# Two encoder layers on one core: the latent heads' first score products are kept in PSUM, their maxima are taken from them by DVE, and the list of the stage is made by readiness

## The chip, the core and the metric

The program runs on one core of a Trainium2 chip. A core has five engines that run their own lists in order and wait for each other by semaphores: TensorE (PE; its weight loads are shown as PEld), VectorE (DVE), ScalarE (ACT), GpSimd (POOL) and SyncE (SP, which here only issues transfers). PE writes to PSUM, which this kernel uses as eight banks of 128 x 512 float32. The metric is the device time of one execution in microseconds (us), as a median over runs.

## The reference

Two layers over 512 tokens of width 1024, batch 1, float32. Each layer normalises its input, projects it, and runs three branches that are merged by gates; then a gated MLP follows. What bears on the change is the first branch, attention from latents with 8 heads of width 96 (64 plain and 32 rotary), cut to its core:

```python
q = (rms_norm(c_q, q_norm_g) @ w_uq).reshape(b, s, MLA_HEADS, MLA_QK)
kv = (rms_norm(c_kv, kv_norm_g) @ w_ukv).reshape(b, s, MLA_HEADS, MLA_NOPE + MLA_V)
k_nope, v = kv[..., :MLA_NOPE], kv[..., MLA_NOPE:]
k = jnp.concatenate([k_nope, k_rope], axis=-1)      # k_rope: one for all heads
q, k = rms_norm(q, qh_g), rms_norm(k, kh_g)         # then axial rotary on the last 32
sc = jnp.einsum('bqgrd,bkgd->bgrqk', q, k) * 96 ** -0.5
p = jax.nn.softmax(sc, axis=-1)
o = jnp.einsum('bgrqk,bkgv->bqgrv', p, v)
# merged = sum over branches of sigmoid(gate) * (o @ w_branch);  x = x + merged @ w_out
# x = x + (silu(conv(hf @ w_up)_gate) * conv(hf @ w_up)_val) @ w_down
```

The second branch is grouped-query attention with 8 heads of width 64 ("gqa" in the code), the third a pooling branch.

## The kernel before

All activations lie with features on partitions and the 512 tokens along the free axis. Every float32 operand is split into a high part that PE takes exactly and a low remainder (ACT copies the high part, DVE or POOL subtracts), and a product is three PE products: high by high, high by low, low by high (`mm3`). Weights stream from HBM through three raw tiles, are split on the core (ACT `wh`, POOL or DVE `wl`), and are used once.

The list of every engine is fixed when the program is built. A small planner, `Clock` (line 133), keeps a model of the time at which each engine is free and each value ready. `chain` (line 184) puts a series of steps on the engines one after another; `Engine` prices each step (0.07 us plus 0.00105 us per element for a DVE step with two inputs, a reduction or a turn; 0.00053 per element for a DVE copy in SBUF), and `mm` prices a product at columns/2370 us, which is 0.216 us for 512. `copy` (line 507) takes ACT or DVE, whichever the model has free sooner, and `pick` does so for DVE and POOL.

The attention of a layer is made by `attention(kind, fill, ...)` (line 1150), first for "gqa", then for "mla", the latent heads. Between its products PE takes units of `fill`: products of the gates and of the branch projections, three 512-wide products a unit, in the two banks called acc. For the latent heads the filler is `fb` (line 1460): the rest of the second branch and the first 48 units of the first branch's gates. What is left of the first branch follows the attention (`rest[0].finish()`, line 1465).

A latent head h goes through these steps:

- `go_turn`: DVE turns 32x32 blocks of the head's q and k (`block_turn`, line 1117; source tiles MQ and MK), SP writes them out and reads them back with features on partitions (`tf`), and a constant `pad` fills partitions 96 to 127: zeros for q, and for k a row of ones at 96 and zeros below it.
- `t_q`, `t_k`: ACT and POOL split them: `qa`, `qb` (high and low of q), `kh`, `kl` (high and low of k; `ka`, `kb` inside the head's record).
- `s_max(h, b)` (line 1232), four times: one product with queries on partitions, `qa` block by `kh`, into the one bank S; DVE reduces it to the negated maximum over keys (`nm`). After the fourth, DVE turns the four columns into `nmt`, and ACT copies them in four steps into partitions 96 to 127 of `qa`.
- `probs(h, k)` (line 1264), four times: three products with keys on partitions, into a bank ST or mi. The ones of the k pad times the maxima in `qa` subtract the maximum inside the product. Then ACT takes the exponential in place (`ex`), ACT or DVE makes the high part `ph`, DVE the low part `pl`, and one value step (`rest`, into `vt`) adds what the 128-column value product leaves out; then the bank is free.
- `av_hi`, `av_lo`, `av_rest`: products with the values into a bank AV; then `o_out` (line 1335) evacuates (ACT), and for each pair of heads the sums are turned, inverted and multiplied (`osum`, `oinv`, `oraw`), and split into `oh`, `ol`.

The order of these steps on PE comes from `PLAN` (line 47): for each kind of head, fixed positions of each step relative to the head's place, in quarters of a head; filler is spread over the positions, and where a step would wait by the model, up to `SLACK` units of filler are taken early. `nbank` (line 297) gives the banks: acc 2, S 1, ST 2, AV 2, mi 1.

The norm of a layer's input (`norm_begin`, line 474) has DVE turn the summed squares into `sqT` and reduce them to `prt`.

Of the kernel before, what the change touches and what calls it, by code (L numbers as in the profile page):

```python
# [13 lines left out]
AF = mybir.ActivationFunctionType  # L14
# [32 lines left out]
PLAN = {"gqa": (-4.2, -1.0, -0.2, 0.0, 0.65, 2.411, 4.57, 32.003),  # L47
        "mla": (-6.2, -2.9, -1.0, 0.1, 0.64, 1.678, 1.82, 35.5)}
# [85 lines left out]
class Clock:  # L134
# [5 lines left out]
    def __init__(self):  # L140
        self.now, self.n, self.heap, self.busy = 0.0, 0, [], False
        self.fin, self.free, self.ready = 0.0, {}, {}
        self.source = self.last = None

# [39 lines left out]
    def chain(self, *steps, after=0.2):  # L184

        def go(n, source=None):
# [77 lines left out]
def trunk(ctx: ExitStack, tc: tile.TileContext, x, w, prm, gb, cst, pad, out):  # L264
# [3 lines left out]
    at, need, done, chain = ck.at, ck.need, ck.done, ck.chain  # L268
# [49 lines left out]
    def f(ap):  # L318
        return ap.bitcast(F32)
# [154 lines left out]
    def norm_begin(gen, sq):  # L474

        t, part = slot("sqT"), small("prt", [P, 16])
# [72 lines left out]
    def layer(l, sq, xsrc):  # L549
# [204 lines left out]
        def set_keys():  # L754
            for _, kb in KAB:
                G.memset(f(kb[64:P, :T]), 0.0)
                G.memset(f(kb[64:65, :T]), 1.0)
# [128 lines left out]

        def gates(br, okey, odst, mode):
            hold = {}

            def gate(m):  # L890
                tag = "AV" if br == 2 and m < 2 else "acc"
                acc = ps(tag)
                yield from feat_major(acc, G1)
                t = hold[m] = slot("gt")

                def logits():
                    V.tensor_tensor(t[:, :T], acc, nrm["rbc"][:, :T], ALU.mult)
                    free(tag)

                chain(([("rbc", G1)], logits), lambda: A.activation(t[:, :T], t[:, :T], AF.Tanh, scale=0.5))  # L900

            def branch(m):
# [22 lines left out]

                if mode == "first":
                    chain(product)
                elif mode == "add":
                    chain(product, add)
                else:  # L930
                    mh, ml = slot("mgh", F32R), slot("mgl", F32R)
                    merged[m] = (mh, ml)
                    chain(product, add, *split(mh[:, :T], ml[:, :T], XM[:, m, :]), fin)
# [47 lines left out]
        def q_out(g, b, acc):  # L981
# [10 lines left out]
            chain(copies, lambda: A.activation(j[:, :384], MQ[g][:, b].rearrange("p h f -> p (h f)"), AF.Square), sums)  # L992
# [55 lines left out]
        def n_out(g, p, acc):  # L1048
# [7 lines left out]
            def sums():  # L1056
# [4 lines left out]
                                               MK[g][:, bs, :, 0:64], AF.Square), sums)  # L1061
# [55 lines left out]
        def block_turn(what, h, srcs, n, rest=None):  # L1117
# [24 lines left out]
            return turn_blocks, put, get  # L1142
# [7 lines left out]
        def attention(kind, fill, okey, odst):  # L1150
# [5 lines left out]

            def t_q(h):
# [7 lines left out]
                def lo():  # L1165
# [3 lines left out]
                chain(lambda: A.activation(qf[:, :T], qf[:, :T], AF.Copy, scale=gcol),  # L1169
                      lambda: A.activation(qa[:, :T], qf[:, :T], AF.Copy), lo, after=0.0)  # L1170
# [92 lines left out]

            def probs(h, k):
# [10 lines left out]
                else:  # L1275
                    mm(sc, s["kb"][:, kb_], s["qa"][:, :T], True, False)
                    mm(sc, s["ka"][:, kb_], s["qb"][:, :T], False, False)
                    mm(sc, s["ka"][:, kb_], s["qa"][:, :T], False, True)
                ph, pl = slot("ph", F32R), slot("pl", F32R)
# [13 lines left out]
                def rest():  # L1293
# [8 lines left out]
                    free(tag)  # L1302
                    if k == 3:
                        done(*key("t", h))

                chain(ex, hi, lo, ([("vg", l, k) if gqa else ("vm", l, k, h // 4)], rest))
# [22 lines left out]
            def av_rest(h):  # L1329
                s = hs[h]  # L1330
                need(key("t", h))
                mm(s["av"], unit, s["t"][:, :T], False, True)
                o_out(h)

            def o_out(h):
# [26 lines left out]
                steps = [copies]  # L1362
                if h % 2 == 1:
# [4 lines left out]
                    steps += [lambda: V.transpose(turned[:, :T], sums[:, :T]),  # L1368
# [3 lines left out]
                    steps += [lambda: V.transpose(sums[:, :T].rearrange("p (b f) -> p b f", f=32),  # L1372
                                                  bc(inv.unsqueeze(2), [P, 16, 32]))]
# [4 lines left out]

            plan = []
# [15 lines left out]
            def waits(fn, h, k=None):  # L1395
# [15 lines left out]
                return [key("t", h)] if fn is av_rest else [key("pl", h, k)], None  # L1411
# [50 lines left out]
        while not ck.has(("tq", l, 0)) and fb.step():  # L1462
            pass
        attention("mla", fb, "om", omla)
# [311 lines left out]
```

## Time and profile before

| | |
|---|---|
| median of three runs | 1565.33 us (1565.16 to 1565.37) |
| span of the profiled execution | 1562.8 us (the page gives its time as this span) |
| instructions | 20576, of them 7098 PE products |
| PE busy | 1556.6 us |
| POOL, DVE, ACT busy | 1035.8, 946.2, 821.5 us |
| granted TensorE clock | 1.000 |
| latent heads, layer 0 | 230.4 to 342.8 us |
| latent heads, layer 1 | 1005.6 to 1118.0 us |

The page names an instruction by line, engine, operation and tiles, output first. Nearly every step here is recorded by a helper (line 379 is every product, 225 every ACT step, 232, 236, 240, 244, 248 and 256 the kinds of DVE and POOL steps), so one goes by the tiles: `nm`, `qb`, `ph`. PE products are pipelined: the length shown of one, 390 ns, is more than the distance from one to the next.

### The profile page before, as it was taken

The page shows a single profiled execution, that of the slowest core. Times are in us where ns is not written, and L with a number is a line of the kernel's source. Part 1 is how long each engine was busy: PE and PEld are TensorE (multiplying, and loading weights), DVE is VectorE, ACT ScalarE, POOL GpSimd, SP SyncE. Part 2 cuts the span into 40 slices and gives each one's busy share as a digit, 9 for nine tenths or more (in the row PEclk, how much of TensorE's full clock was granted, in tenths as well). Part 3 has the DMA queues.
Part 4 walks back from the last instruction along what each step waited for, and adds up shares of the span by engine and source line. Part 5 has one row for each costly group of instructions (what it writes and reads, how often), then busy time and mean ns, then how long its engine had stood idle before and what let it go on. Part 6 is the DMA issues. An engine that isn't in the chain of part 4 may idle for free.

```text
span 1562.8 us, 20576 instructions
## 1 busy us (share of the span) xinstructions
PE 1556.6 (100%) x7098; PEld 1301.2 (83%) x7098; DVE 946.2 (61%) x1377; ACT 821.5 (53%) x1538; POOL 1035.8 (66%) x922
## 2 busy tenths in 40 slices
PE   9999999999999999999999999999999999999999
PEld 8888788888888888888898888888888888888888
DVE  6778877865266777711046788788562767776000
ACT  6558777863444444432244687788533444444221
POOL 4975985854667666664578669867546676666542
PEclk9999999999999999999999999999999999999999
DMA  6432234325323323333335322443242222322331
GB/s 208 125 109 75 75 117 151 111 68 149 96 93 108 95 94 95 95 120 111 112 105 135 95 77 73 141 137 101 82 149 94 94 95 95 107 95 95 108 130 46
DMA packets 82856, 166.48 MB, mean 107 GB/s; under 512 B 20928, under 2 KB 42944, under 8 KB 82752
## 3 DMA queue, kind: packets, MB, share of 16 engines
q1 hardware_dynamic: 82464, 165.03, 33.8%
q8 instruction: 56, 0.92, 0.2%
q14 instruction: 48, 0.39, 0.1%
q10 hardware_dynamic: 288, 0.14, 0.0%
HBM read 151.50 MB, written 13.63 MB: 106 GB/s over the span
## 4 chain that ended last, share of the span: by engine, by line
PE 97%; POOL 2%; issue 0%; DMA 0%; ACT 0%; SPq 0%; DVE 0%; POOLq 0%
PE ps_acc L379 44%; PE ps_AV L379 23%; PE ps_ST L379 22%; PE ps_mi L379 3%; PE ps_S L379 3%; POOL MQ L232 0%; DMA XM<-x 0%; POOL wl L232 0%; POOL oraw L232 0%; POOL qb L232 0%; POOL qa L232 0%; SPq L330 0%; SPq L1606 0%; POOL rp L232 0%; ACT HH L225 0%
## 5 line engine op out<-in xcount | busy, mean ns | idle before, releaser
L232 POOL TENSOR_TENSOR wl<-raw,wh 128x512 fp32r<-128x512 f32 (+3 forms) x503 | 675.4, 1355 | 369.5 <-ACT wh L225 336.4
L225 ACT ACTIVATE wh<-raw 128x512 fp32r<-128x512 f32 (+2 forms) x521 | 308.2, 607 | 124.8 <-PE ps_ST L379 42.7
L236 DVE SCALAR_TENSOR_TENSOR a<-u,prm,a 128x511 f32<-128x511 f32 x176 | 243.1, 1384 | 91.8 <-ACT a L225 87.8
L379 PE MATMUL ps_acc<-HH,wh 128*128 128x512 f32 x592 | 231.1, 390 | 0.1
L379 PE MATMUL ps_acc<-HL,wh 128*128 128x512 f32 x592 | 230.9, 390 | 0.0
L379 PE MATMUL ps_acc<-HH,wl 128*128 128x512 f32 x592 | 230.8, 390 | 0.0
L379 PEld LDWEIGHTS ps_acc<-HH,wl 128*128 128x128 f32 x592 | 111.2, 188 | 23.3
L379 PEld LDWEIGHTS ps_acc<-HH,wh 128*128 128x128 f32 x592 | 111.3, 188 | 22.8 <-issue 0.4
L379 PEld LDWEIGHTS ps_acc<-HL,wh 128*128 128x128 f32 x592 | 111.2, 188 | 22.6
L232 POOL TENSOR_TENSOR al<-a,ah 128x512 fp32r<-128x512 f32 x44 | 58.1, 1320 | 83.5 <-ACT ah L225 81.4
L379 PE MATMUL ps_AV<-HH,wh 128*128 128x512 f32 x288 | 112.4, 390 | 0.0
L379 PE MATMUL ps_AV<-HH,wl 128*128 128x512 f32 x288 | 112.2, 390 | 0.0
L379 PE MATMUL ps_AV<-HL,wh 128*128 128x512 f32 x288 | 112.2, 390 | 0.0
L240 DVE TENSOR_REDUCE nm<-ps_S 128x1 f32<-128x512 f32 x128 | 87.6, 684 | 37.0 <-PE ps_S L379 36.5
L225 ACT ACTIVATE ah<-a 128x512 fp32r<-128x512 f32 x44 | 27.8, 632 | 128.1 <-DVE a L232 128.1
L379 PE MATMUL ps_ST<-HH,wh 128*128 128x512 f32 x240 | 93.6, 390 | 0.0
L379 PE MATMUL ps_ST<-HL,wh 128*128 128x512 f32 x240 | 93.5, 390 | 0.0
L379 PE MATMUL ps_ST<-HH,wl 128*128 128x512 f32 x240 | 93.5, 389 | 0.0
L225 ACT ACTIVATE a<-u,prm 128x512 f32<-128x512 f32 x88 | 71.0, 809 | 23.8 <-DVE u L232 23.5
L225 ACT ACTIVATE a<-a 128x512 f32<-128x512 f32 x44 | 27.6, 632 | 104.4 <-DVE a L236 104.3
L225 ACT ACTIVATE HH<-XM,prm 128x512 fp32r<-128x512 f32 x32 | 23.1, 722 | 102.9 <-DVE XM L232 53.9
L225 ACT ACTIVATE ps_ST<-ps_ST 128x512 f32<-128x512 f32 x86 | 50.1, 583 | 28.5 <-PE ps_ST L379 28.4
(387 smaller groups left out, 3752.3 us busy)
## 6 DMA issues: line engine op xcount, KB each, us to landing
raw<-w SPq DMA_DIRECT2D x228, 512.0 KB, 3.5
raw<-w SPq DMA_DIRECT2D x13, 384.0 KB, 3.1
XM<-x SPq DMA_DIRECT2D x16, 256.0 KB, 3.8
dtq<-tr SPq DMA_DIRECT2D x16, 192.0 KB, 1.9
dtk<-tr SPq DMA_DIRECT2D x16, 192.0 KB, 2.2
tf<-dtq SPq DMA_DIRECT2D x48, 64.0 KB, 2.2
tf<-dtk SPq DMA_DIRECT2D x48, 64.0 KB, 2.1
raw<-w SPq DMA_DIRECT2D x6, 448.0 KB, 3.4
```

The lines of the kernel that those rows point to most:

```text
L225: return self.eng.activation(out, in_, func, **k)
L232: return self.eng.tensor_tensor(out, *a)
L236: return self.eng.scalar_tensor_tensor(out, *a)
L240: return self.eng.tensor_reduce(out, in_, *a, **k)
L379: PE.matmul(o, lhsT=lhsT, rhs=rhs, start=start, stop=stop)
```

## The change

Only the latent heads and the norm's reduction are rewritten; grouped-query heads keep `PLAN` and `s_max`.

- `a_part(h, k)` takes the place of `s_max` and of one of the three products of `probs`: high by high, keys on partitions, into one of the banks ST, ST, mi, S, or one of the two AV banks if no other score holds one. The bank is kept. DVE reduces each bank with a reduction that turns 32x32 blocks (`largest`), so that the maximum over 32 keys of a query lands on a partition; after the fourth, `over_keys` (a small reduction over the four banks), `gather` (three DVE copies of 16 elements, from the other groups of 32 partitions to partitions 96 to 127), `over_groups` (a small reduction, negated) and `row` (a DVE product of that with a 32x32 identity, 32 x 512, into partitions 96 to 127 of `qb`).
- `pad` for k is ones in all 32 rows, so that the product of k with the diagonal blocks in `qb` subtracts each query's maximum.
- `b_part(h, k)` adds the other two products to the bank (high k by `qb`, low k by `qa`), then the same steps as before (`weights`). The value steps of one head now wait for each other in the planner's order.
- `held_banks` takes the place of the fixed positions: it goes over a list of tasks, in order of heads, and issues the first that the model has ready, with a margin (0.1 us for `a_part`, 0.4 for `b_part`, 1.2 for the value products); if none is, a unit of filler. A head's first `a_part` waits until a share of the filler is done, with 22 units left for after the last head's start.
- `low` and `way` mark steps that give way in the planner: if their engine is busy by the model, they are put off, up to 4 us (1 us for the filler's bank steps, 1.5 for the evacuation of values).
- `norm_begin` uses one reduction that turns, in place of turn and reduction.

```diff
-PLAN = {"gqa": (-4.2, -1.0, -0.2, 0.0, 0.65, 2.411, 4.57, 32.003),
-        "mla": (-6.2, -2.9, -1.0, 0.1, 0.64, 1.678, 1.82, 35.5)}
+PLAN = {"gqa": (-4.2, -1.0, -0.2, 0.0, 0.65, 2.411, 4.57, 32.003)}
+LEAD = {"mla": (1.2, 22)}
...
+    def low(self, fn, most=4.0, engine="DVE"):
+        self.gives_way[fn] = (engine, most)
+        return fn
...
+            eng, most = self.gives_way.get(fn, (None, 0.0))
+            since = self.now if since is None else since
+            if self.free.get(eng, 0.0) > self.now + 0.02 and self.now < since + most:
+                self.at(self.free[eng] - self.now, lambda: go(n, source, since))
+                return
...
-        chain(([("sq", gen, kc) for kc in range(KC)], lambda: V.transpose(t[:, :T], sq[:, :T])),
-              lambda: V.tensor_reduce(part, t[:, :T].rearrange("p (j r) -> p j r", r=32), AX.X, ALU.add),
+        chain(([("sq", gen, kc) for kc in range(KC)], lambda: V.tensor_reduce(
+            part, sq[:, :T].rearrange("p (j r) -> p j r", r=32), AX.X, ALU.add, apply_transpose=True)),
...
+        def way(br, fn, most=4.0):
+            return low(fn, most) if now_mla[0] else fn
...
+            def a_part(h, k):
+                s = hs[h]
+                tag, sc = sc_bank()
+                s["sc", k] = (tag, sc)
+                PE.matmul(sc, lhsT=s["ka"][:, k * P:k * P + P], rhs=s["qa"][:, :T], start=True, stop=True)
...
+                def largest():
+                    V.tensor_reduce(s["pm"][:, k], sc.rearrange("p (j r) -> p j r", r=32), AX.X, ALU.max,
+                                    apply_transpose=True)
+
+                def over_keys():
+                    s["row"] = small("mrow", [P, 16], bufs=1)
+                    V.tensor_reduce(s["pk"][:, 3], s["pm"].rearrange("p k j -> p j k"), AX.X, ALU.max)
+
+                def gather():
+                    for g in range(4):
+                        if 32 * g != base:
+                            V.tensor_copy(s["pk"][base:base + 32, g if g < 3 else base // 32], s["pk"][32 * g:32 * g + 32, 3])
+
+                def over_groups():
+                    V.tensor_reduce(s["row"][base:base + 32], s["pk"][base:base + 32].rearrange("p g j -> p j g"), AX.X, ALU.max,
+                                    negate=True)
+
+                def row():
+                    V.tensor_tensor(s["qb"][base:base + 32, :T].rearrange("p (j r) -> p j r", r=32),
+                                    bc(s["row"][base:base + 32].unsqueeze(2), [32, 16, 32]),
+                                    bc(ident[base:base + 32, None, base:base + 32], [32, 16, 32]), ALU.mult)
+                    done(*key("m", h))
+
+                chain(largest, *[over_keys, gather, over_groups, ([key("q", h)], row)] * (k == 3), after=0.3)
+
+            def b_part(h, k):
+                s = hs[h]
+                need(key("m", h), key("q", h))
...
+                pairs = [("kb", "qb")] if gqa else [("kb", "qa"), ("ka", "qb")]
+                for n, (a_, b_) in enumerate(pairs):
+                    PE.matmul(sc, lhsT=s[a_][:, kb_], rhs=s[b_][:, :T], start=False, stop=n == len(pairs) - 1,
+                              skip_group_check=True)
+                    ck.to(ck.now + T / 2370.0)
+                weights(h, k, sc, lambda: sc_free(tag))
...
-                chain(ex, hi, lo, ([("vg", l, k) if gqa else ("vm", l, k, h // 4)], rest))
+                chain(ex, hi, lo, ([("vg", l, k) if gqa else ("vm", l, k, h // 4)] + [key("t", h, k - 1)] * (k > 0), rest))
...
+            def held_banks():
...
+                lead, late = LEAD[kind]
+                step = (fill.total - fill.done - late) / 7.0
...
+                    for k in range(4):
+                        task(a_part, h, k, keys=[key("q" if gqa else "qh", h)] + [key("kh", h)] * (not gqa), margin=0.1, bank="sc",
+                             after=[(t_q, h - h % 2 if gqa else h)] + [(b_part, h - 1, 3)] * (h > 0) + [(t_k, h)] * (not gqa)
+                             + [(a_part, h, k - 1)] * (k > 0), fills=f0 + step * h if k == 0 else 0)
+                    for k in range(4):
+                        task(b_part, h, k, keys=[key("m", h), key("q", h)] + [key("kl", h)] * (not gqa), margin=0.4,
+                             after=[(b_part, h, k - 1) if k else (a_part, h, 3)])
...
+                while todo:
+                    for n, z in enumerate(todo):
+                        if can(*z):
+                            todo.pop(n)
+                            z[0](*z[1])
+                            issued.add((z[0],) + z[1])
+                            break
+                    else:
+                        if not fill.step():
+                            ck.to(ck.now + 0.05)
+                fill.finish()
...
-        "pad": np.stack([np.zeros((32, T), np.float32), np.eye(32, 1, dtype=np.float32) * np.ones(T, np.float32)]),
+        "pad": np.stack([np.zeros((32, T), np.float32), np.ones((32, T), np.float32)]),
```

More of the change, by code (lines that the diff above doesn't have):

```diff
@@ L267, in trunk @@
     ck = Clock()
-    at, need, done, chain = ck.at, ck.need, ck.done, ck.chain
+    at, need, done, chain, low = ck.at, ck.need, ck.done, ck.chain, ck.low
     V, A, G = Engine(ck, nc.vector, "DVE"), Engine(ck, nc.scalar, "ACT"), Engine(ck, nc.gpsimd, "Pool")
@@ L924, in fin @@
                     done("mrg", l, m)
+                way(br, product, 1.0)
                 if mode == "first":
@@ L990, in sums @@
                 done("ssq", l, g, b)
-            chain(copies, lambda: A.activation(j[:, :384], MQ[g][:, b].rearrange("p h f -> p (h f)"), AF.Square), sums)
+            chain(copies, lambda: A.activation(j[:, :384], MQ[g][:, b].rearrange("p h f -> p (h f)"), AF.Square), way(0, sums))
         def q_norm(g):
@@ L1140, in get @@
                 done(what, l, h)
-            return turn_blocks, put, get
+            return way(0, turn_blocks), put, get
         def mla_turn(what, h):
@@ L1155, in key, with sc_tags, sc_ready, sc_bank @@
                 return (kind, l) + k
+            held = [0]
+            def sc_tags():
+                return ("ST", "mi", "S") + ("AV",) * (held[0] == 0)
+            def sc_ready():
+                return any(banks[t] and banks[t][0] <= ck.now for t in sc_tags())
+            def sc_bank():
+                while not any(banks[t] for t in sc_tags()):
+                    ck.pop()
+                tag = min((t for t in sc_tags() if banks[t]), key=lambda t: max(banks[t][0], ck.now) + 0.01 * (t == "AV"))
+                held[0] += tag == "AV"
+                return tag, ps(tag)
+            def sc_free(tag):
+                held[0] -= tag == "AV"
+                free(tag)
             def t_q(h):
@@ L1278, in probs, with weights @@
                     mm(sc, s["ka"][:, kb_], s["qa"][:, :T], False, True)
+                weights(h, k, sc, lambda: free(tag))
+            def weights(h, k, sc, release):
+                s = hs[h]
                 ph, pl = slot("ph", F32R), slot("pl", F32R)
@@ L1360, in add @@
                     G.tensor_tensor(raw[:, :T], raw[:, :T], sums[:, :T], ALU.add)
-                steps = [copies]
+                steps = [low(copies, 1.5, "ACT") if kind in LEAD else copies]
                 if h % 2 == 1:
@@ L1379, in attention @@
+            if kind not in PLAN:
+                held_banks()
+                return
             plan = []
```

74 lines of the change are left out of this document (59 added, 15 removed).

## Prediction

> **What bounds the kernel now.** I read the page's busy times and its chain first, then the chain in order of time, then windows over the two latent-attention stages, and there what TensorE's weight loads wait for. First the busy times and the chain's shares by engine, from the page.
>
> ```profile
> PE 1556.6 (100%) x7098; PEld 1301.2 (83%) x7098; DVE 946.2 (61%) x1377; ACT 821.5 (53%) x1538; POOL 1035.8 (66%) x922
> PE 97%; POOL 2%; issue 0%; DMA 0%; ACT 0%; SPq 0%; DVE 0%; POOLq 0%
> ```
>
> PE is never free and 97% of the chain is PE: time is the number of products times their rate. The chain in order of time (start, length, how many products) gives the rate, and the borders of the stages.
>
> ```profile
> 217.32 13.07 PE ps_acc L379 x63
> 342.82 37.40 PE ps_acc L379 x165
> 663.72 14.96 PE ps_acc L379 x66
> 992.60 13.05 PE ps_acc L379 x63
> 1118.00 37.40 PE ps_acc L379 x165
> ```
>
> 14.96/66 = 0.2267 us for one 512-wide product (the 390 ns shown for one is its pipelined length). In layer 0 the latent heads stand between the filler that ends at 230.4 and the run of 165 that starts at 342.8; in layer 1 between 1005.6 and 1118.0. Busy times of the two stages, and of the even middle of the first:
>
> ```profile
> core 0: us, PE busy (x) PEld busy (x) DVE busy (x) ACT busy (x) POOL busy (x), PEclk, DMA share, GB/s
> 230.00:343.00 113.00, 113.00 (x498) 93.12 (x497) 86.07 (x145) 86.08 (x171) 75.72 (x64) 1.00 0.38 114
> 1005.00:1118.00 113.00, 113.00 (x498) 93.16 (x497) 86.07 (x145) 85.92 (x170) 76.05 (x64) 1.00 0.36 115
> 245.00:330.00 85.00, 85.00 (x376) 70.05 (x375) 69.48 (x120) 71.18 (x143) 59.76 (x51) 1.00 0.35 107
> ```
>
> PE has no gap there, at full granted clock; DVE is at 76%, POOL at 67% (82% and 70% in the middle). What the weight loads waited for in the first stage comes to 0.7 us:
>
> ```profile
> PEld ps_ST L379 <- issue: 0.3, 1, 0.3
> PEld ps_mi L379 <- ACT qa L225: 0.2, 1, 0.2
> PEld ps_AV L379 <- DVE vt L236: 0.2, 1, 0.2
> ```
>
> **Removed.** The products of the row maxima, from the groups by shape:
>
> ```profile
> L379 PE MATMUL ps_S<-kh,qa 128*128 128x512 f32 x64 | 25.0, 390 | 0.0
> ```
>
> They recompute a product that the scores need anyway; the change computes it once. 64 x 0.2267 = **14.5 us** less PE work, 7.25 in each stage, all of it on the chain.
>
> **Off the path.** ACT loses four copies per head and DVE the turn of the maxima; the 64 reductions become 64 that also turn 32x32 blocks. Rows by tile, and the two groups that bear on a reduction that turns:
>
> ```profile
> L225 ACT ACTIVATE qa<-nmt x64: 305/308/312, 239.3 to 1099.5; 32x128 fp32r<-32x128 f32 x64
> L256 DVE STREAM_TRANSPOSE nmt<-nm x32: 291/302/314, 108.3 to 1098.1; 128x128 f32<-128x128 f32 x32
> L240 DVE TENSOR_REDUCE nm<-ps_S x128: 626/684/695, 101.8 to 1097.4; 128x1 f32<-128x512 f32 x128
> L256 DVE STREAM_TRANSPOSE sqT<-sq 128x512 f32<-128x512 f32 x4 | 2.8, 712 | 8.4 <-POOL sq L232 8.3
> L240 DVE TENSOR_REDUCE prt<-sqT 128x16 f32<-128x512 f32 x4 | 2.7, 686 | 0.1
> L240 DVE TENSOR_REDUCE rt<-fac 128x4 f32<-128x16 f32 x4 | 0.7, 170 | 0.1
> ```
>
> A turn alone is 0.71 and a reduction alone 0.68; both in one pass is at least 0.68 and at most 1.40. I take 0.69, since each is one pass over 512 elements. The norm's merged step (four in the program) can save up to 4 x 0.71 us of DVE that PE does not wait for; I put it at nothing, and its cover is the filler in front of the forced finish. The new order between the value steps (a head's step k after step k-1, both kinds of heads) costs nothing: DVE took them in that order before.
>
> Steps that give way may come later. The gates' and branches' bank steps wait at most 1 us; a bank of acc is asked for again after one other tile, four units of 3 x 0.2267 = 2.7 us at the least. The turns of the next head's q and k wait at most 4 us, and with them the ten transfers each pair issues on SP's queue; the row of the page for most of them:
>
> ```profile
> tf<-dtq SPq DMA_DIRECT2D x48, 64.0 KB, 2.2
> ```
>
> The new list asks for a turn a whole head (about 13 us) ahead, so 4 us and two landings of some 2 us fit; weight loads behind them on SP come up to as much later, covered by three raw tiles. Nothing for both; if that cover goes, q of the next head is late next.
>
> **New on the path: the chain to the maximum.** All of a head's second and third products wait for the row in qb. From the start of the head's fourth first product: 0.39 (product) + 0.69 (reduction) + two small reductions (0.17 for 16 elements; 0.22 each for 64, an estimate) + three copies of 16 elements + the row step, 32x512 with two SBUF inputs. The nearest rows for the last two, min/median/max in ns:
>
> ```profile
> L244 DVE TENSOR_SCALAR y<-ssm x4: 172/182/674, 154.0 to 963.2; 128x32 int32<-128x32 int32 x4
> L232 DVE TENSOR_TENSOR win<-win,C x16: 153/168/1252, 36.7 to 840.2; 128x8 f32<-128x8 f32 x16
> L232 DVE TENSOR_TENSOR a<-a,a x44: 691/693/1662, 448.9 to 1443.3; 128x512 f32<-128x512 f32 x44
> L236 DVE SCALAR_TENSOR_TENSOR a<-u,prm,a x176: 737/1657/1891, 441.4 to 1441.6; 128x511 f32<-128x511 f32 x176
> ```
>
> At their floors: copies 3 x 0.16, row 0.69, and some 0.3 between steps: 0.39 + 0.69 + 0.44 + 0.48 + 0.69 + 0.3 = 3.0 us. The planner, by its own prices (0.07 + 0.00105 per element for two-input and reducing steps), sees 0.216 + 0.3 + 0.608 + 0.137 + 0.235 + 0.137 + 0.608 + four gaps of 0.13 + 0.15 = 2.91, adds the margin 0.4, and rounds up to a filler unit (half of 3 x 0.216: 0.32): 3.63. It prices a product at 0.216, so PE really spends 3.63 x 0.2267/0.216 = 3.81 us there. **Cover: 0.8 us per head.** What is queued behind the wait is everything: PE takes its list in order.
>
> But the maxima of those rows lie far above their floors. Three rows that follow each other on DVE, and what POOL ran then, from the timeline:
>
> ```profile
> 78.35 1.22 DVE L236 SCALAR_TENSOR_TENSOR yt<-yt,y 128x32 f32<-128x32 f32 x1
> 79.60 1.22 DVE L236 SCALAR_TENSOR_TENSOR y<-yt,y 128x32 f32<-128x32 f32 x1
> 80.85 1.22 DVE L232 TENSOR_TENSOR yt<-y,ssr 128x32 f32<-128x32 f32 x1
> 77.46 5.81 POOL L232 TENSOR_TENSOR wl<-raw,wh 128x288 fp32r<-128x288 f32 x5
> ```
>
> A DVE step on SBUF alone can sit out a whole POOL step. The old maxima read PSUM (626 to 695 ns, no spread); the four new ones per head do not, and POOL then turns to the next head's qb and kl, which are let go right behind the fourth first product. The extra per step is bounded by nothing (median of win) and by about 1.1 us (its maximum less its floor). Means, as groups:
>
> ```profile
> L244 DVE TENSOR_SCALAR y<-ssm 128x32 int32<-128x32 int32 x4 | 1.2, 302 | 0.2 <-POOL ssm L244 0.2
> L232 DVE TENSOR_TENSOR win<-win,C 128x8 f32<-128x8 f32 x16 | 7.6, 516 | 13.8 <-POOL win L232 13.7
> L236 DVE SCALAR_TENSOR_TENSOR oraw<-osum,warm,oraw 128x512 f32<-128x512 f32 x4 | 3.8, 938 | 0.0
> L232 DVE TENSOR_TENSOR oraw<-oraw,osum 128x512 f32<-128x512 f32 x4 | 3.3, 816 | 0.1
> L232 DVE TENSOR_TENSOR XM<-XM,gt 128x512 f32<-128x512 f32 x16 | 19.3, 1207 | 0.4
> L236 DVE SCALAR_TENSOR_TENSOR a<-u,prm,a 128x511 f32<-128x511 f32 x176 | 243.1, 1384 | 91.8 <-ACT a L225 87.8 <-POOL wl L232 1.0
> ```
>
> The least extra is nothing: a step cannot pass its floor. Extras of the means over the floors: 0.13, 0.36, 0.20, 0.12, 0.52 and 0.65 us. The first five are tiny steps or stand at the end of a latent stage; their mean is 0.27. Four steps give 1.1 us a head; less the cover, 0.3; 16 heads: **+4.8 us**.
>
> **New on the path: banks.** The next head's first products wait for banks that this head's last value steps let go, with a margin of only 0.1. DVE's real 0.684 is 12% above the plan's 0.608, PE's 0.2267 5% above its 0.216, so over some six DVE steps in a row DVE falls back 6 x (0.684 - 0.608 x 1.05) = 0.27 us. Between nothing (the rounding to filler units hides it; a gain is excluded, as PE waits only 0.7 us there now) and 0.27 x 16 = 4.3 us, no row is nearer to one end; I take half, **+2.2**.
>
> **Sum.** 1562.8 - 14.5 + 4.8 + 2.2 = 1555.3 as a span. The page gives no other time of its execution; the median of the runs, 1565.33, lies 2.5 above the span, so the forecast is **1557.8 us**, 0.5% faster. Later stages keep their lists; weights land as before, since no new transfer is issued.
>
> **Rivals.**
>
> *Nothing stalls*: the copies slip in before POOL starts qb, and the row hits a gap. For it: win's median is its floor. 1565.3 - 14.5 = 1550.8.
>
> *Each of the four steps waits out the POOL step in flight.* POOL's steps there, by tile:
>
> ```profile
> L232 POOL TENSOR_TENSOR qb<-tf,qa x16: 1277/1294/1311, 227.8 to 1086.3; 128x512 fp32r<-128x512 f32 x16
> ```
>
> At POOL's 70% the wait is 0.70 x 1.29/2 = 0.45 a step, 1.8 a head, a stall of 1.0: 16 us, with the banks 18.2, against 14.5: 1569.0. [...] The timeline above agrees; the medians at the floor in a<-a,a and win show how often it does not bite, so I don't take it for the forecast.
>
> *As in the feed-forward (slower).* If every step pays the 0.65 of a<-u,prm,a, where POOL is kept busy beside DVE, it is 2.6 a head, a stall of 1.8, 28.8 us, plus 2.2: 1581.8. Sign changes where (14.5 - 2.2)/16 + 0.8 = 1.57 us a head, 0.39 us a step; the rows lie on both sides of that.
>
> *DVE becomes the bound.* In the middle 85 us, from the groups there:
>
> ```profile
> L240 DVE TENSOR_REDUCE nm<-ps_S 128x1 f32<-128x512 f32 x26 | 17.8, 683 | 6.2 <-PE ps_S L379 6.2
> L248 DVE CAST ph<-ps_ST 128x512 fp32r<-128x512 f32 x5 | 3.4, 676 | 3.6 <-ACT ps_ST L225 3.6
> L248 DVE CAST ph<-ps_mi 128x512 fp32r<-128x512 f32 x3 | 2.0, 672 | 0.3 <-ACT ps_mi L225 0.3
> ```
>
> 26/4 = 6.5 heads, so a head takes 13.1 us of PE and 10.7 of DVE. After: PE 13.1 - 0.9 = 12.2; DVE 10.7 - 0.3 + 0.44 + 0.48 + 0.69 + 1.1 = 13.1. That is 0.9 too much, 14.4 us in 16 heads: 1565.2. Against it: the planner puts each ph on the freer engine, and ACT loses 4 x 0.31 us a head; with the 5.4 us of casts (0.8 a head) gone from DVE, the two are even.
>
> *A reduction that turns is two passes*: 64 x 0.71 = 45 us more of DVE, 2.8 a head, on engines that were even: 1550.8 + 45 = 1596.
>
> **How the numbers follow.** The forecast with its neighbours, 1550.5 to 1562.0, has 0.50, of which the case without stalls is 0.18; DVE full, or the lock at the mild end of its rival, near no change 0.15; the lock at 1568.5 and above, with the feed-forward case, 0.23; lock and full DVE together, slower, 0.07; two passes 0.05. 0.2% (3.1 us) is about what a measurement of this kernel tells from no change: faster 0.51, same 0.14, slower 0.35. The range runs to the feed-forward rival's lower half, 1578, leaving about a tenth above it.
>
> **What would show it.** PE has 64 records fewer, and the tile nm of the latent heads is gone. The turning reduction stands at 0.69; if at 1.4, the last rival holds. [...] The first products waiting on DVE's value steps: the bank term. The three copies and the row step spread from their floor to above 1.2 us, with a POOL step over each long one. DVE above 95% of the shortened stage: the bound has moved. I am wrong if the runs of filler end before the last head does, so that PE waits at the end of the stage.

## The result and the profile after

The kernel with the change takes 1574.5 us (median of four runs, 1572.1 to 1575.3), the kernel before 1565.2 us in the runs beside it. The ratio is 1.0058, with a 95% interval of 1.0044 to 1.0073: slower by 0.58%, or 9.3 us. 1557.8 us was forecast. The profiled execution has a span of 1570.3 us, 7.5 above the 1562.8 of before.

Busy times and the chain's shares by engine, from the page of the changed kernel:

```profile
PE 1548.3 (99%) x7034; PEld 1288.0 (82%) x7034; DVE 1008.8 (64%) x1471; ACT 788.6 (50%) x1460; POOL 1032.4 (66%) x918
PE 30%; DVE 4%; ACT 0%; issue 0%; DVEq 0%
```

The 64 products are gone (7098 less 7034). But PE stood idle for 1570.3 - 1548.3 = 22.0 us, where it was 6.2 before, and DVE was busy for 63 us more. The chain can be followed back for a third of the span only (30 + 4%), to about 1020 us in the second latent stage; DVE, which held none of it before, holds 4% there. The same windows over the two latent stages that the prediction read (columns as there):

```profile
core 0: us, PE busy (x) PEld busy (x) DVE busy (x) ACT busy (x) POOL busy (x), PEclk, DMA share, GB/s
230.00:343.00 113.00, 106.17 (x458) 84.79 (x456) 110.51 (x189) 67.48 (x127) 73.88 (x62) 1.00 0.39 117
1005.00:1118.00 113.00, 105.19 (x450) 84.37 (x450) 110.04 (x186) 66.95 (x126) 74.00 (x63) 0.98 0.41 123
```

PE was busy for all 113 us of each. It now idles 6.8 and 7.8 us there, 14.6 in both, and a product takes 106.17/458 = 0.232 and 105.19/450 = 0.234 us, where 113/498 = 0.227 stood before: over 908 products some 5 us more. The granted clock is 1.00 in the first stage and 0.98 in the second, so the clock is not all of it; what the rest is, no row shows. So -14.5 for the products, +14.6 and +5 make +5 of the 7.5; the rest is spread over the program. DVE is at 98% of the first stage (76% before). What PE waited for, over the whole program (total us, times, longest):

```profile
PE ps_ST L1348 <- DVE qb L242: 6.8, 4, 1.9
PE ps_AV L1348 <- DVE qb L242: 4.8, 4, 1.9
PE ps_S L1348 <- DVE qb L242: 1.5, 2, 0.9
```

L1348 holds the second and third products, and qb on DVE is the row of maxima. These 13.1 us are the stall that the prediction had at 4.8. The weight loads (PEld) of the same products wait 13.6 us for qb, in 9 waits of up to 2.3. The steps of the chain to the row, as groups (busy us, mean ns of one | idle us before them):

```profile
L258 DVE COPY nmt<-nmt 32x16 f32<-32x16 f32 x48 | 36.1, 752 | 1.0
L250 DVE TRANSPOSE_TENSOR_REDUCE nmt<-ps_ST 128x16 f32<-128x512 f32 x28 | 19.3, 695 | 0.5 <-PE ps_ST L1307 0.4
L242 DVE TENSOR_TENSOR qb<-mrow,C 32x512 fp32r<-32x512 f32 x16 | 11.8, 737 | 1.1
L250 DVE TENSOR_REDUCE mrow<-nmt 32x16 f32<-32x64 f32 x16 | 4.2, 260 | 0.5
```

The reduction that turns is one pass, 0.695 us. A copy of 16 elements takes 752 ns in the mean; by tile, its minimum, median and maximum:

```profile
L258 DVE COPY nmt<-nmt x48: 167/982/1316, 234.4 to 1120.1; 32x16 f32<-32x16 f32 x48
```

The timeline of DVE and POOL around one head's copies, and the first and the last row step of the first stage (start, length, engine, how many):

```profile
235.89 0.69 DVE L242 TENSOR_TENSOR qb<-mrow,C 32x512 fp32r<-32x512 f32 x1
...
278.84 1.59 DVE L258 COPY nmt<-nmt 32x16 f32<-32x16 f32 x3
279.11 1.29 POOL L242 TENSOR_TENSOR wl<-raw,wh 128x512 fp32r<-128x512 f32 x1 [4.64 <-ACT wh L235]
...
342.40 0.69 DVE L242 TENSOR_TENSOR qb<-mrow,C 32x512 fp32r<-32x512 f32 x1
```

Three copies at their floor would have ended at 279.34. They end at 280.43, with the POOL step that began between them (279.11 + 1.29 = 280.40). Counted over the whole trace, the 16 copies at 167 to 169 ns began with no POOL step in flight; each of the other 32 began under one and ended 27 to 35 ns after its end.

From the first to the last row step there are (342.40 - 235.89)/7 = 15.22 us a head. I call this the round: row, second and third products, exponentials, weights and value steps on DVE, bank free, next head's first products, their reductions, next row. The chain in order of time shows one of the second stage, from the last reduction of one row (mrow) to that of the next (start, length):

```profile
1074.11 0.27 DVE mrow L250
...
1075.12 0.69 DVE wl L242
1075.81 0.95 DVE tr L266 x2
...
1078.53 0.60 DVE pl L242
1079.12 0.62 DVE nmt L250
...
1081.62 0.66 DVE vt L246
1082.28 0.62 DVE nmt L250
...
1086.35 0.98 DVE nmt L258
...
1087.35 1.23 DVE nmt L258
...
1088.60 1.23 DVE nmt L258
...
1089.85 0.27 DVE mrow L250
```

But for about 1 us shown as gaps between steps, all of its 15.74 us are DVE, one step behind the other, with the copies (nmt at L258) at 3.4 us among them; PE is not in it. Not every step is the head's own: low parts of weights (wl), turns for a later head (tr) and gates (gt) stand in it too, so in this round DVE had no room. POOL at its three copies:

```profile
1086.01 1.30 POOL L242 TENSOR_TENSOR kl<-tf,kh 128x512 fp32r<-128x512 f32 x1 [1.05 <-ACT kh L235]
1087.26 1.29 POOL L242 TENSOR_TENSOR qb<-tf,qa 128x512 fp32r<-128x512 f32 x1
1088.50 1.28 POOL L242 TENSOR_TENSOR wl<-raw,wh 128x512 fp32r<-128x512 f32 x1
```

Each copy ends just behind a POOL step, and the next copy begins 0.09 us after the start of the next one (1087.26, then 1087.35), so it waits out nearly all of it. Of the 32 copies that waited, 22 began at most 0.11 us after the start of their POOL step.

### The profile page after: what moved, and what is told of

Read it like the earlier page. It is cut to its first block, busy times and chain, and to the rows that moved or that the text cites. A ratio compares the mean times of both kernels' runs of the same rounds, so it can differ in the third digit from the quotient of the medians.

```text
span 1570.3 us, 20451 instructions
## 1 busy us (share of the span) xinstructions
PE 1548.3 (99%) x7034; PEld 1288.0 (82%) x7034; DVE 1008.8 (64%) x1471; ACT 788.6 (50%) x1460; POOL 1032.4 (66%) x918
## 5 line engine op out<-in xcount | busy, mean ns | idle before, releaser
L242 POOL TENSOR_TENSOR wl<-raw,wh 128x512 fp32r<-128x512 f32 (+2 forms) x499 | 671.0, 1356 | 356.5 <-ACT wh L235 331.6
L246 DVE SCALAR_TENSOR_TENSOR a<-u,prm,a 128x511 f32<-128x511 f32 x176 | 246.4, 1401 | 93.0 <-ACT a L235 86.1
L235 ACT ACTIVATE gt<-gt 128x512 f32<-128x512 f32 x48 | 30.2, 630 | 75.5 <-DVE gt L242 73.3
L389 PEld LDWEIGHTS ps_AV<-HH,wl 128*128 128x128 f32 x288 | 54.1, 188 | 11.3
```

What stands on the lines that cost most here:

```text
L235: return self.eng.activation(out, in_, func, **k)
L242: return self.eng.tensor_tensor(out, *a)
L246: return self.eng.scalar_tensor_tensor(out, *a)
L389: PE.matmul(o, lhsT=lhsT, rhs=rhs, start=start, stop=stop)
```

## The experiments

Two theories at the start. *Copies*: three tiny copies a head wait out POOL's steps, and that time costs. *Something else*: the row step, the banks or the new orders cost, and the copies are covered. The kernel before, run beside each set of runs, took 1564.7 to 1565.1 us. In the runs with reductions alone, with extra reductions and with unread copies every engine's list is that of the kernel they start from; in all others the planner makes the orders anew, and a difference can also come from that.

**Reductions in place of the copies.** A reduction over an axis of length 1 moves the same 32x16 elements. The planner is told the copy's price, so all orders stay as in the changed kernel.

```diff
-V.tensor_copy(s["pk"][base:base + 32, g if g < 3 else base // 32], s["pk"][32 * g:32 * g + 32, 3])
+dst = s["pk"][base:base + 32, g if g < 3 else base // 32]
+V._count(dst, 0.00053, 0.07)
+V.eng.tensor_reduce(dst, s["pk"][32 * g:32 * g + 32, 3].unsqueeze(2), AX.X, ALU.max)
```

> The three gathering copies are made as reductions over an axis of length one; the planner is told the old price, so every engine's list stays as in the changed kernel, step by step. Lock theory (the copies of 16 elements take 0.75 us on average because they wait for POOL's step, and that fills DVE and delays the row): the copies fall to about 0.2 us without spread, DVE is given back some 16 x 3 x 0.55 = 26 us, PE's waits for qb go, and the time falls from 1574 to 1551 to 1558. Rival (DVE is full with the turning reductions and the lists made by readiness are too tight in any case): the time stays at 1567 or above and PE still waits for qb.

Measured: 1555.0 us, ratio 0.9937 (0.9922 to 0.9952), so 19.5 us under the changed kernel and faster than before. Its groups, by-tile row, windows, and row steps:

```profile
L1327 DVE TENSOR_REDUCE nmt<-nmt 32x16 f32<-32x16 f32 x48 | 7.8, 162 | 1.0
L242 DVE TENSOR_TENSOR qb<-mrow,C 32x512 fp32r<-32x512 f32 x16 | 16.9, 1059 | 1.1
```

```profile
L1327 DVE TENSOR_REDUCE nmt<-nmt x48: 161/161/165, 233.3 to 1100.5; 32x16 f32<-32x16 f32 x48
L242 DVE TENSOR_TENSOR qb<-mrow,C x16: 686/938/1853, 234.2 to 1101.0; 32x512 fp32r<-32x512 f32 x16
```

```profile
230.00:343.00 113.00, 112.86 (x494) 91.95 (x493) 106.76 (x197) 71.62 (x135) 78.42 (x64) 1.00 0.41 120
1005.00:1118.00 113.00, 112.37 (x491) 91.33 (x490) 104.75 (x188) 74.99 (x143) 78.72 (x63) 1.00 0.37 114
```

```profile
234.20 0.69 DVE L242 TENSOR_TENSOR qb<-mrow,C 32x512 fp32r<-32x512 f32 x1
...
331.94 0.90 DVE L242 TENSOR_TENSOR qb<-mrow,C 32x512 fp32r<-32x512 f32 x1
```

The same move takes 162 ns with no spread, beside a POOL as busy as it was (78.4 us of the first stage, 73.9 in the changed kernel), and 44 of the 48 began with a POOL step in flight: the copy waits for POOL, the reduction does not. 28.3 us of DVE go, of which 5.1 come back in the row step, which now meets the POOL steps itself: in the first stage 7 of its 8 begin with a POOL step in flight, and 6 of these take 0.90 to 1.80 us; in the changed kernel 1 of 8 does, and all take 0.69 to 0.71. PE's idle time in the stages falls from 14.6 to 0.8 us and the round to (331.94 - 234.20)/7 = 13.96. So the three forms differ here: a copy takes 167 to 1316 ns, the row step with its two inputs in SBUF 686 to 1853, a reduction 161 to 165; why POOL holds up the first two and not the third is shown by no row.

**The copies on ACT.** The three gathering copies of a head are made by ACT, and the orders are made anew.

```diff
-V.tensor_copy(s["pk"][base:base + 32, g if g < 3 else base // 32], s["pk"][32 * g:32 * g + 32, 3])
+A.activation(s["pk"][base:base + 32, g if g < 3 else base // 32], s["pk"][32 * g:32 * g + 32, 3],
+             AF.Copy)
```

> [...] Lock theory: ACT takes about 0.21 us for each as for the copies of 32x16 in the evacuation of values, and the time is 1551 to 1560. Rival: 1567 or above.

Measured: 1557.6 us, 0.9953 (0.9938 to 0.9968). A copy takes 0.213 us on ACT (212 to 217 ns). So it is not the form of step that heals: two forms that do not wait for POOL both do.

**The planner told of the wait.** The copies stay, and each counts 0.67 us more.

```diff
 V.tensor_copy(s["pk"][base:base + 32, g if g < 3 else base // 32], s["pk"][32 * g:32 * g + 32, 3])
+ck.took("DVE", 0.67)
```

> The copies stay, but the planner is told 0.75 us for each, what they measured, so that PE's list puts filler in front of the products that wait for the row. If the loss is the unforeseen wait in PE's list alone: PE's waits for qb go and the time is 1553 to 1560. If the loss is DVE's time (98% busy through the stage): DVE stays above 95% and the time at 1568 to 1578, the waits of PE only standing elsewhere.

Measured: 1593.0 us, 1.0180 (1.0165 to 1.0195), the slowest of all, and above both ranges. By tile, and the window behind the first stage:

```profile
L258 DVE COPY nmt<-nmt x48: 166/169/1244, 234.2 to 1141.4; 32x16 f32<-32x16 f32 x48
```

```profile
343.00:381.00 38.00, 31.83 (x113) 23.79 (x113) 25.55 (x42) 17.36 (x34) 14.15 (x12) 0.82 0.14 43
```

In the new order 28 of the 48 copies take 166 to 170 ns (the other 20 take 722 to 1244), and yet the round is 16.29 us, 1.07 more than in the changed kernel: the later rows are in the list. From 230 to 335 us PE is busy for 100.12 of 105 us, 98.17 in the changed kernel; behind that it lacks work (31.83 of 38 us at a clock of 0.82, where the changed kernel has 38.00 at 1.00). So a stall at the row, unforeseen, is not the whole cost: this list, in which the wait is planned, costs more. How much of that is the price and how much the rest of the new order, the run does not tell.

**The norm's merged step alone, on the kernel before.**

```diff
-chain(([("sq", gen, kc) for kc in range(KC)], lambda: V.transpose(t[:, :T], sq[:, :T])),
-      lambda: V.tensor_reduce(part, t[:, :T].rearrange("p (j r) -> p j r", r=32), AX.X, ALU.add),
+chain(([("sq", gen, kc) for kc in range(KC)], lambda: V.tensor_reduce(
+    part, sq[:, :T].rearrange("p (j r) -> p j r", r=32), AX.X, ALU.add, apply_transpose=True)),
```

> The kernel before with the norm's merged turn and reduction alone. By the prediction nothing: 1565.2 +- 1. If the new wait of 1.5 us at the turn of the grouped keys in layer 0 comes from this edit: about 1567.

Measured: 1566.2 us, 1.0010 (1.0000 to 1.0019): 1.5 us more, at the edge of what can be told. A wait that the weight loads of before do not have:

```profile
PEld ps_S L383 <- ACT gt L225: 1.5, 1, 1.5
```

**Reductions, and the norm's two steps as before.** The first experiment with the edit of the last undone.

> As the run with reductions in place of the copies, with the norm's turn and reduction as two steps again. If the norm's edit costs the 1.5 us that it cost alone: 1553 to 1554, against 1555.0. If that was only a shift in one list: 1555 +- 1.

Measured: 1553.2 us, 0.9927 (0.9911 to 0.9944): 12.0 us under the kernel before, and the fastest of all. It is 1.8 us under the first experiment; as that agrees in size with the 1.5, the norm's edit probably costs, though no interval here separates it from nothing: that of the edit alone begins at 1.0000, and those of the two kernels with reductions overlap.

**The same DVE time without POOL, ahead of the row and behind it.** Two kernels on top of the first experiment, each with three reductions a head of 416 elements that nobody reads. Each takes 585 to 589 ns, near what a copy lost (752 - 167 = 585 in the mean), with no wait for POOL; the planner does not count them, and the orders stay. In one they stand among the gathering steps, in the other right behind the row step.

```diff
+V.eng.tensor_reduce(small("dum", [P, 1], bufs=1), C[:, 0:416], AX.X, ALU.max)   # x3 a head
```

> [...] If only the time on the way to the row matters, and not what causes it: the time comes back to that of the changed kernel, 1570 to 1578. If the copies harm in another way, through POOL: 1560 or below.

> The same three extra reductions, but right behind the row step, so that the row is not later and DVE is as full as in the run before this. If DVE's sum is the bound: as with them ahead of the row, 1570 to 1578. If the row's lateness is the bound: 1555 to 1562.

Measured: 1575.4 us, 1.0067 (1.0052 to 1.0082) ahead, and 1574.1 us, 1.0059 (1.0044 to 1.0074) behind: 20.4 and 19.1 us over the first experiment. From the groups and the weight loads' waits of the one behind the row:

```profile
L1339 DVE TENSOR_REDUCE dum<-C 128x1 f32<-128x416 f32 x48 | 28.1, 586 | 1.6
...
PEld ps_ST L1307 <- DVE vt L246: 4.7, 10, 0.7
```

28.1 us of DVE, the copies' excess (48 x 0.585), cost what the copies cost, with POOL out of it, and cost the same where the row is not late by them. Behind the row it is the next head's first products (L1307) that wait, for banks that value steps (vt) free late. So the price is neither the row's lateness alone nor any delay to POOL's steps. Both times fit a bound by DVE's sum, which is taken up below.

**Three unread copies in the kernel before.** Behind the turn of the maxima, 32x16 each.

```diff
+if not gqa:
+    scr = small("scr", [P, 16], bufs=1)
+    for g in range(3):
+        V.eng.tensor_copy(scr[96:128], C[32 * g:32 * g + 32, 0:16])
```

> The kernel before, with three copies of 32x16 a latent head added on DVE behind the turn of the maxima, into a scratch tile that nobody reads; the planner is not told. It prices the same instructions where DVE has slack (76% busy). If the copies cost through the stage that they sit in (held banks, full DVE): they show the same spread, about 0.17 to 1.3 us, and the time moves by less than 3 us, to 1565 to 1568. If such copies cost by themselves, by holding POOL up: 1570 or above.

Measured: 1578.2 us, 1.0085 (1.0070 to 1.0100): 13.0 us, a miss for the thought that the old order has room. From the groups and the weight loads' waits:

```profile
L1253 DVE COPY scr<-C 32x16 f32<-32x16 f32 x48 | 26.7, 556 | 1.6
...
PEld ps_AV L379 <- DVE pl L232: 10.0, 10, 2.2
```

26.7 us of DVE at 0.49 us of time for each. The time lies where copies that hold POOL up were expected, but POOL's steps are as long as before: the largest group (wl, 503 steps) has a mean of 1357 ns, 1355 in the kernel before. In the old order the value products wait (ps_AV for pl): 24% of DVE's time is free in the stage, but, it seems, not between the steps of a head.

**Is the bound DVE's sum?** The step that rounds the softmax weights (ph), which goes to the freer engine, is put always on ACT in the latent heads, by a bias against DVE: once in the changed kernel, once in the fastest one.

```diff
-copy(ph[:, :T], sc)
+copy(ph[:, :T], sc, bias=C_BIAS if gqa else 9.0)
```

> The changed kernel with its copies as they are, but the high part of the weights of latent heads always made by ACT (60% busy in the stage) and not by whichever of ACT and DVE the planner holds free sooner. That takes 17 casts of 0.67 us a stage, 11.4 us, from DVE, nearly what the copies lose there (24 x 0.59 = 14 us), and leaves the copies on the way to the row. If DVE's sum is the bound, as the extra reductions before and behind the row say: 1556 to 1563. If the late row is: 1570 to 1576.

> Reductions in place of the copies, the norm's step as before, and the high parts on ACT. With DVE's sum as the bound there is little left to win at 94% of DVE: 1551 to 1553, against 1553.2 without the move; the floor by PE's products alone is 1550.8. If the new lists are worse: 1555 or above.

Measured: 1584.1 us, 1.0129 (1.0113 to 1.0145), and 1564.3 us, 0.9999 (0.9990 to 1.0009). DVE got free and both became slower, the first beyond either range. The first stage of the first, and behind it; then a window of the second:

```profile
230.00:343.00 113.00, 106.72 (x461) 86.43 (x460) 98.51 (x166) 74.28 (x142) 72.13 (x62) 0.98 0.38 118
350.00:365.00 15.00, 12.04 (x33) 8.02 (x34) 8.33 (x13) 9.21 (x18) 4.38 (x3) 0.77 0.09 27
```

```profile
335.00:350.00 15.00, 11.89 (x34) 7.52 (x33) 10.28 (x19) 10.32 (x20) 3.87 (x4) 0.78 0.13 35
```

DVE falls from 110.5 to 98.5 us of 113, and PE still idles 6.3 us there and 3.0 of 15 in the window behind. What DVE waited for in the first stage, in the first kernel and in the second:

```profile
DVE pl L242 <- ACT ph L235: 10.3, 11, 2.0
```

```profile
DVE pl L242 <- ACT ph L235: 13.2, 14, 2.2
```

Neither wait is there in the changed kernel or in the fastest one: the time that DVE was given went into waiting for ACT. So the two runs do not show what a DVE with less work would have done in the changed kernel. They show that in these lists DVE's sum is not the bound. The rounds (below) grow by 0.86 and 0.74 us, and the copies add about as much to a round with ph on ACT (16.08 - 14.85 = 1.23) as between the same two kernels without it (15.22 - 14.11 = 1.11): the two add up, as times in one line do, though DVE now has room. The chain over the second stage (1030 to 1120 us, by line) of the first of the two shows where the step went:

```profile
by line: DVE nmt L258 17.5%; DVE nmt L250 14.4%; DVE vt L246 11.8%; DVE pl L242 7.5%; issue 6.2%; ACT ph L235 5.5%; DVE qb L242 3.9%; DVE gt L242 3.9%; DVE gt L246 3.2%; DVE tr L266 2.9%; ACT ps_ST L235 2.4%; DMA tf<-pad 2.1%; DVE wl L242 2
```

ph is in the chain still, on ACT (5.5%): it changed its engine, not its place in the round. Why ACT makes it later than DVE did was not tried.

**Four banks in place of five**, in the fastest kernel: same steps, same DVE work, one bank less for held scores and value sums.

```diff
-return ("ST", "mi", "S") + ("AV",) * (held[0] == 0)
+return ("ST", "mi", "S")
```

> Reductions in place of the copies, the norm's step as before, and no score in an AV bank: four banks for the held scores and not five, DVE's work unchanged. If the round of a head through the held banks is the bound (row step to row step 14.1 us with five banks, 15.2 in the changed kernel): the round grows by one value step or more, to 15 us or above, and the time by about 14 rounds of that, to 1563 to 1580, with DVE less busy than 94% in the stage. If DVE's sum is the bound: 1553 to 1556 and DVE at 93% or above.

Measured: 1561.7 us, 0.9982 (0.9973 to 0.9992): 8.6 us lost with one bank less, between the two ranges, with DVE as busy (106.1 us of the first stage, 106.5 with five banks) and PE at 111.65:

```profile
230.00:343.00 113.00, 111.65 (x483) 90.00 (x482) 106.12 (x196) 70.19 (x131) 78.09 (x64) 1.00 0.40 119
```

**No giving way**, in the fastest kernel.

```diff
-return low(fn, most) if now_mla[0] else fn
+return fn
...
-steps = [low(copies, 1.5, "ACT") if kind in LEAD else copies]
+steps = [copies]
```

> Reductions in place of the copies, the norm's step as before, and no step gives way any more. The prediction put giving way at nothing: 1553 +- 1. If it is what keeps the held banks short on a DVE that is 94% busy: 1556 to 1565.

Measured: 1567.4 us, 1.0017 (1.0008 to 1.0027), so giving way is worth 14.2 us here, more than either range had. DVE is less busy than with it (99.9 us of the first stage, 106.5 with it). The end of the first stage:

```profile
335.00:350.00 15.00, 10.44 (x34) 6.79 (x33) 11.96 (x23) 7.18 (x13) 3.83 (x3) 0.89 0.10 35
```

**All rounds.** First and last start of a row step in the first stage, from each timeline as above; the round is their distance by 7.

| kernel | first, last row (us) | round (us) | time (us) |
|---|---|---|---|
| reductions | 234.20, 331.94 | 13.96 | 1555.0 |
| reductions, old norm | 232.76, 331.52 | 14.11 | 1553.2 |
| copies on ACT | 234.88, 334.95 | 14.30 | 1557.6 |
| four banks | 232.89, 334.26 | 14.48 | 1561.7 |
| reductions, ph on ACT | 232.78, 336.76 | 14.85 | 1564.3 |
| no giving way | 235.20, 340.46 | 15.04 | 1567.4 |
| the change | 235.89, 342.40 | 15.22 | 1574.5 |
| extra reductions ahead of the row | 235.83, 342.92 | 15.30 | 1575.4 |
| extra reductions behind the row | 234.01, 341.78 | 15.40 | 1574.1 |
| the change, ph on ACT | 236.53, 349.12 | 16.08 | 1584.1 |
| copies priced | 239.48, 353.49 | 16.29 | 1593.0 |

Both columns rise together, but for neighbours that change places within 2 us (the first two, and the change with the two of the extra reductions). Copies to reductions shorten seven rounds of the first layer by 106.51 - 97.74 = 8.8 us; in the second layer, between the same steps (1012.63 to 1120.61 and 1002.77 to 1100.99), it is 107.98 - 98.22 = 9.8, together 18.5 of the 19.5 us. So the length of a head's round orders the times, whether DVE, ACT or a bank makes it longer. As the stage is eight such rounds, the table says that the time is lost within it, not by what: that is for the edits to say. Nor can it tell how much of each round is planned and how much is waiting.

## Why the prediction was wrong

**The saved products: right.** 64 fewer, and the kernel without the copies' waits and with the old norm lies at 1553.2: 2.5 us above 1565.2 - 14.5 = 1550.7.

**The turning reduction and the small ones: right.** 0.695 measured, 0.69 taken; 0.26 for the small ones, 0.22 taken. The rival of two passes is out.

**"Their mean is 0.27": the step that failed.** The mechanism, DVE steps that wait out POOL's, was named, and its size was taken as the mean of five groups elsewhere in the program. Measured, the four steps of the changed kernel pay (3 x (752 - 167) + (737 - 687))/4 ns = 0.45 us each in place of 0.27, beyond the 0.39 at which the prediction had the sign turn. The extra of one copy, 0.585 us, is near the 0.65 of the feed-forward row, and that of the row step near nothing. The rival in which each of the four steps waits out the POOL step in flight put 0.45 on a step, and its 1569.0 came nearest; it was set aside for medians at the floor, while the copies' own median is 982 ns. That its 0.45 is the measured mean is in part luck: it took half a POOL step at 70% for all four, where three paid 0.585 and one 0.05, and a copy that follows one that waited meets the next POOL step at its start and waits out nearly all of it, not half (22 of the 32 that waited began at most 0.11 us after that start). No run shows the lock that the chances speak of; the runs showed copies of 167 to 169 ns with no POOL step in flight, and of 234 to 1316 ns under one, which ended 27 to 35 ns after its end.

**"Cover: 0.8 us per head": wrong in kind.** Four extras of 0.45 less that cover give 1.0 us a head, 16 us, and 1569.0 in all. 5.5 us more were measured. The cover was worked out for the row alone, as if DVE time mattered only by making the row late. The extra reductions behind the row, which cost as much as those ahead of it, show that DVE time counts elsewhere in the round too: 0.69 us of time for each us of the copies' excess (19.5/28.1), 0.73 and 0.68 in the two kernels with extra reductions. That part of it was covered stays right; what covers the remaining third, no run shows.

**The bank term, +2.2: fair as a size.** By the sign named for it, the weight loads of first products (L1307) wait 1.7 us for value steps (vt) in the changed kernel and 3.4 in the fastest one. The 2.5 us that remain of the fastest kernel's sum hold that, and the row's own waits too; the runs do not part them.

**The norm's edit at nothing: probably wrong by 1 to 2 us** (+1.5 alone, 1.8 in the pair). With 2.5, 1.8 and 19.5 the sum is -14.5 + 23.8 = +9.3, as measured; the first of these is a remainder, so the sum closes by itself.

**Giving way at nothing: wrong.** It was looked at only for what it delays. In the fastest kernel it shortens the round by 0.93 us (15.04 to 14.11) and is worth 14.2 us: without it even that kernel is 0.17% slower than before. In the changed kernel itself it was not taken away.

**The rival of a full DVE: half.** DVE was to pass 95% and did (98%), and the copies' time is DVE time. In the round shown of the second stage DVE had no room at all, and the extra reductions fit its sum. But four banks and no giving way make the round longer on a DVE that is no fuller (106.1 and 99.9 us of 113), and with ph on ACT, at 87%, it waits. So a full DVE describes the changed kernel; whether its sum or the line of steps through the banks is what binds there, the runs do not part. And the sign by which the prediction would be known to be wrong, PE waiting at the end of the stage, shows in other kernels (priced copies, ph on ACT, no giving way, four banks). The changed kernel itself lost its time within the stage, at the row.

## What to carry over

A tiny DVE copy between SBUF tiles can be priced by what POOL runs beside it, not by its size (here 167 to 1316 ns for 16 elements), and several in a row can each pay a whole POOL step (1.23 us a copy beside steps of 1.29): look at the median in the place where it will stand, or choose a form that did not wait here, such as a reduction over an axis of one (161 to 165 ns). Where a few banks are held from one head's step to the next, measure the round from one such step to the next and count what is added to it, wherever it stands (here 0.7 us for each us of DVE); an engine's share of busy time says neither that there is room nor that it is the bound. Removing work from PE paid here only where the round stayed short: 12.0 us of the 14.5 in the fastest kernel, less than nothing in the changed one.

## What was not expected

- Three unread copies of 16 elements a head cost the kernel before 13.0 us, although DVE was at 76% there.
- The copies shield the row step: with them it takes 737 ns in the mean, with reductions 1059. In the first stage one row step of 8 begins under a POOL step with the copies, 7 of 8 with reductions.
- Where PE idles at the end of a stage, its granted clock can fall in the same window: 0.77, 0.78 and 0.89 in the 15 us windows above, 0.82 over 38 us, where the kernel before has 1.00 in the same places. It does not always: with four banks PE is busy for 12.53 of the 15 us from 335, at 1.00. In the window at 0.82 a product takes 31.83/113 = 0.282 us, in the kernel before 37.88/168 = 0.225 over the same 38 us; whether the waiting lowers the clock, and how much of the longer product is the clock, no run shows.
- Priced at their measured cost, 28 of the 48 copies stay at their floor (166 to 170 ns), and the kernel is the slowest of all. Why that order keeps them there was not tried.
